# Bias-tile loads, last-pair store tiles and one product's place at the seam between a projection stage and an attention stage

## The chip, the cores and the metric

The kernel runs on 1 core of one Trainium2 chip. The metric is the time of one execution on the device, in microseconds (us). Engines are named as in the profile: PE multiplies matrices, DVE and ACT work elementwise, POOL issues software DMAs (and does a little elementwise work), SP issues hardware DMAs. Each engine runs its instructions in the order in which they stand in its program; a semaphore wait at the head stops everything behind it on that engine.

## The reference, cut to what matters

A transformer block on 1024 tokens of width 1024, all in float32. One projection makes every input of two mixers and the merge gates; the second mixer (NSA) is attention in three branches with a relative-position bias.

```python
u = rms_norm(h, g_norm_mix[l])
proj = jnp.einsum('btd,de->bte', u, w_in[l]) + b_in[l]        # 1024 x 5408
mq, mk, mv, mo, mi, mf, nq, nkv, ngate, merge = split_columns(proj, IN_SIZES)
y_m = mlstm_mixer(mq, mk, mv, mo, mi, mf, ...)
y_n = nsa_mixer(nq, nkv, ngate, pe_cmp[l], w_cmp1[l], w_cmp2[l], rel_bias)
...
# in nsa_mixer, per block of queries:
lc = q @ kc_ + table[rel_bucket(t - cmp_end)];   p_c = masked_softmax(lc, ...)
ls = q @ k_g + bias_s;                           p_s = masked_softmax(ls, ...)
lw = q @ k_wb + table[rel_bucket(dist)];         p_w = masked_softmax(lw, mask_w)   # window of 512
out = gb[0] * (p_c @ vc_) + gb[1] * (p_s @ v_g) + gb[2] * (p_w @ v_wb)
...
gates = jax.nn.sigmoid(merge); mixed = jnp.sum(gates * branch, axis=2)
```

## The kernel before, in words

Activations and weights are split into a high and a low float32r part, and each product is three matmuls (lines 351 to 353: high by high, high by low, low by high). The normalised, transposed activations lie in two tiles, `UTH` and `UTL`.

**The projection stage** makes 128-column tiles of the projection in pairs (the table `PAIRS`, numbered 0 to 11; pairs 10 and 11 are merge gates 0 to 3). A pair is computed by a seven-product 2x2 block scheme: products 1 to 7, in the order 1, 6, 2, 7, 4, 5, 3. The left operand is a block of `UTH`/`UTL` or one of four operands derived from them. Products 1, 2, 3 read blocks in place, 5, 6, 7 read the derived operands in the T tiles, and product 4 reads the fourth derived operand, which has been written over one quarter of `UTH`/`UTL`; the quarter's own values wait in DRAM (`d_b12`) and are loaded back by POOL (line 1335, eight loads of 256 KB) once the last product 4, that of pair 11, has been read. The right operand is a weight block or a sum of them, prepared by ACT (high part, line 723) and DVE (low part, line 494) into a ring of four operand tiles `op0` to `op3`. Raw weights come through a ring of three tiles `rp0` to `rp2`. A product takes 12 matmuls and one of eight PSUM banks (`bk0` to `bk7`); the results are evicted in the order of the products: product 1 by ACT (line 779), the others by DVE (lines 776 and 786), into the pair's two 1024-column destination tiles. For pairs 7 to 11 these are the tiles S0 and S1. Once complete they are stored to DRAM by SP: pair 9 to `d_qh`/`d_ql` (lines 1040 and 1041), pairs 10 and 11 to `d_mg` (line 1045).

The order of the work in this stage is set by a planner (`Plan`): steps with reads, writes, costs and a rank are put greedily on the engines, and a step that raises its `boost` goes ahead. `preps` prepares operands some products ahead of the one that is planned, in the order of `plist`. `compress` (four weight tiles in S4 to S7, lines 1211 to 1248) runs between the products.

**The seam.** While the last products run, the attention stage's inputs are loaded: by POOL the queries (S4, S5), keys (S8, S9 and R10) and values, by SP the bias tiles of the first pair of heads (`load_f`, line 1301: S6 and S7, 1024 columns each, from `d_rep`). `first_merge` prepares the first merge weight tile for the next stage (line 1346 load, 1349 and 494 split). After the plan the windowed bias tiles `FW0` and S2 (640 columns each) are loaded by SP.

**The attention stage** has 32 units (a pair of heads and a block of 128 queries), in an order written out by its own scheduler, filled up with merge products (`d`, lines 351 to 353). Logits of a unit go to one of two PSUM tiles `S` (lines 1430 and 1431); DVE adds the bias and takes the row minimum (line 1457, `E...<-S...`), which frees the PSUM tile; ACT takes the exponential (1461); DVE scales (1482); PE transposes (1512); ACT and DVE split (1517, 1521); PE multiplies by the values (1532, 1534). Unit 0 (query block 0) reads S6 and S7; unit 1 (query block 7) reads `FW0` and S2 first.

Of the kernel before, what the change touches and what calls it, by code (L numbers as in the profile page):

```python
# [8 lines left out]
F32 = mybir.dt.float32  # L9
# [5 lines left out]
P = 128  # L15
T = 1024
# [15 lines left out]
FX = 1152  # L32
# [140 lines left out]
def body(ctx, tc, a, out):  # L173
    nc = tc.nc
# [48 lines left out]
    S = {n: Region(bigp, f"S{n}", 1024, F32R if n < 2 or n > 3 else F32) for n in (0, 1, 4, 5, 6, 7, 8, 9)}  # L223
# [9 lines left out]
    def slot(n):  # L233
        return S[n]() if n < 10 else R10()[:, 1024 * (n - 10):1024 * (n - 9)]
# [56 lines left out]
    d_mg = [tc.dram_tile([P, T], F32, name=f"d_mg{j}") for j in range(16)]  # L291


    class Stream:
# [12 lines left out]
        def dma(self, upto):  # L307
            while self.nd <= min(upto, len(self.jobs) - 1):
                src, (n, m), _ = self.jobs[self.nd]
                t = self.pool.tile([P, T], F32, name=f"raw{self.nd}", tag="raw", bufs=self.bufs)  # L310
                v = t[:, 0:n * m].rearrange("p (n m) -> p n m", n=n)
                col = 0
                for s in (src if isinstance(src, list) else [src]):
                    w = s.shape[-1]
                    nc.sync.dma_start(v[:, :, col:col + w], s)
                    col += w
                self.raw[self.nd] = v
                self.nd += 1
# [76 lines left out]
    def fm_tile(n, psp, dtag, dbufs, evict, pool=False, deep=False, mark=False):  # L395

        wh, wl = ws.get(n)
        for r in range(2):
            ps = psp.tile([P, 512], F32, name=f"d{n}_{r}", tag=dtag, bufs=dbufs)
            for k in range(KT):  # L400
# [51 lines left out]

    PAIRS = [("qk", 0), ("kw", 0), ("qk", 1), ("cv", 0), ("qk", 2), ("o", 0), ("qk", 3), ("nq", 0),
             ("o", 2), ("nq", 2), ("mg", 0), ("mg", 2)]
    DSLOT = [11, 0, 11, 0, 11, 0, 11, 0, 0, 0, 0, 0]
    HSLOT = {1: lambda r: slot(6 + r), 7: lambda r: slot(11 + r), 9: lambda r: (RND, RMV)[r]()[:, 0:1024]}
    HKEY = {1: lambda r: keys_of(6 + r), 7: lambda r: keys_of(11 + r), 9: lambda r: [("ND", "MVH")[r]]}
    DBI = {"qk": lambda j: j, "o": lambda j: 4 + j // 2, "cv": lambda j: 6, "kw": lambda j: 7,
# [49 lines left out]
    def sbuf(*ns):  # L508
        return pl.buf([k for n in ns for k in keys_of(n)], True)
# [289 lines left out]
    LAST = NPR - 1  # L799
    SEQ = {n: [(n, q) for q in (1, 6, 2, 7, 4, 5, 3)] for n in range(NPR)}  # L800
# [1 line left out]
    SEQ[1] = [(1, q) for q in (6, 7, 4, 5, 3)]  # L802
    SEQ[LAST] = [(LAST, q) for q in (4, 1, 6, 2, 7, 5, 3)]
    plist = [x for n in range(NPR) for x in SEQ[n]]
    made = []

    def preps(upto):
        while len(made) < min(upto, len(plist)):
            n, q = plist[len(made)]
            prep(n, q)  # L810
            made.append((n, q))
            if q == 3:
                load_raw(n + 2, 0)
            for m in (n, n + 1):
                if (m, 1) in made and (m == 0 or (m - 1, 3) in made) and (m, 3) not in SB_:
                    for s in (1, 2, 3):
                        sums(m, s)
                    load_raw(m + 1, 1)
# [104 lines left out]
    for t in (1, 2, 3):  # L923
        for j in range(4):
            x = pl.buf([("T", t, j)], True)
# [15 lines left out]
    for j in range(4):  # L941
        b = tf1[j]
# [3 lines left out]
    for j in range(4):  # L946
        b = tf2[j]
# [3 lines left out]
    for j in range(4):  # L951
        tsplit(1, j, f1(j), tf1[j])
        b = tf1[j]
# [3 lines left out]
    for j in range(4):  # L957
        b = tf2[j]
# [13 lines left out]
    drep = pl.buf((), True)  # L972
# [17 lines left out]
    dkc, dkk, dym = pl.buf((), True), pl.buf((), True), pl.buf((), True)  # L990
    dqq = [pl.buf((), True) for _ in range(4)]
    dmg = pl.buf((), True)
# [31 lines left out]
    def finish(n):  # L1024
        nm, j = PAIRS[n]
        d = DST[n]
        rows_ = [[d[r, 0], d[r, 1]] for r in range(2)]
        if nm == "qk":
            pl.boost = -60
            conv(n)  # L1030
            pl.boost = 0
        elif nm in ("kw", "nq"):
            for r in range(2):
                v = lambda r=r: slot(DSLOT[n] + r)
                hb, hi = pl.buf(HKEY[n](r), True), lambda r=r: rnd(HSLOT[n](r))
                dh, dl = (d_kh[r], d_kl[r]) if nm == "kw" else (d_qh[j + r], d_ql[j + r])
                tok = dkk if nm == "kw" else dqq[j + r]
                step1("ACT", 1000.0, lambda hi=hi, v=v: nc.scalar.activation(hi(), v(), AF.Copy), rows_[r], [hb])
                ew(ANY2, lambda v=v: rnd(v()), v, lambda hi=hi: cast32(hi()), ALU.subtract, [hb], rows_[r])
                dma(lambda dh=dh, hi=hi: nc.sync.dma_start(dh, cast32(hi())), [hb], [tok])  # L1040
                dma(lambda dl=dl, v=v: nc.sync.dma_start(dl, v()), rows_[r], [tok])
        else:
            for r in range(2):
                d_ = {"cv": d_kc[r], "o": d_so[(j + r) % 4], "mg": d_mg[j + r]}[nm]
                dma(lambda d_=d_, r=r: nc.sync.dma_start(d_, slot(DSLOT[n] + r)), rows_[r], [dkc] if nm == "cv" else [dmg])


    def head(h):
# [206 lines left out]
    fbt = lambda r: S[6 + r]()  # L1255
# [39 lines left out]

    def load_f(p, r, w, eng):
        h = 2 * p + r
        t_, o_, n_ = (fbt(r), 127, T) if not w else (FWT(r), FX + 127, 640)
        (FW if w else FB)[h] = t_
        d_ = d_rep[h][0:1, :]  # L1300
        eng.dma_start(t_, bass.AP(tensor=d_.tensor, offset=d_.offset + o_, ap=[[RW - 1, P], [1, n_]]))
# [15 lines left out]
    def first_loads():  # L1317
# [9 lines left out]
        dma(lambda: load_f(0, 1, 0, nc.sync), [drep], [b[7]])  # L1327
        gl(4, lambda: load_k(0, 0, gq), [dkk], [b[8], b[9]])

    def last_loads():  # L1330
        nd, mv, sm = pl.buf(["ND"], True), pl.buf(["MVH"], True), pl.buf([("ss", z) for z in range(2)] + [("CN", z) for z in range(3)], True)
        for z, b in ((1, nd), (2, mv), (3, sm)):
            gl(1, lambda z=z: load_v(z), [dvh], [b])
        for j in range(4):
            gl(2, lambda j=j: [nc.gpsimd.dma_start(FS[4][z][:, :, j], d_b12[z][:, :, j]) for z in range(2)], [db12], tb[4, j])
        b = sbuf(3)
        gl(1, lambda: load_v(0), [dvh], [b])
        gl(1, lambda: load_v(4), [dvh], [pl.buf((), True)])
# [21 lines left out]
    for n in range(NPR):  # L1360
        for x in SEQ[n]:
            pl.boost = 80
            preps(plist.index(x) + 4)
            pl.boost = 0
            product(*x)
            if x[1] == 3:
                if n == 0:
                    rel_rows()
                finish(x[0])
                nm, j = PAIRS[x[0]]  # L1370
                if nm == "qk":
                    head(j)
        if n == 8:
            compress()
        if n == LAST - 1:
            first_loads()
# [15 lines left out]
    with ExitStack() as sc:  # L1392
        cp = sc.enter_context(tc.tile_pool(name="stC", bufs=1, reuse_waits="tile"))
        psC = sc.enter_context(tc.tile_pool(name="psC", bufs=1, space=PSUM, reuse_waits="tile"))
        FWT = {0: cp.tile([P, 640], F32, name="FW0"), 1: S[2]()}.__getitem__
        for r in range(2):
            load_f(0, r, 1, nc.sync)


        def c_dense():  # L1400
# [319 lines left out]
        while any(queues.values()):  # L1720
            best = None
            for e in queues:
                cand = None
                for op in queues[e][:LOOK[e]]:
                    r = ready(op, e)
# [74 lines left out]
    with ExitStack() as se:  # L1800
# [32 lines left out]
        for d in range(8):  # L1833
            n = j_br[d]
# [155 lines left out]
    for i in range(NT):  # L1990
        b = piece(16 + i)
# [252 lines left out]
    for gi, pairs in enumerate(GROUPS):  # L2244
# [6 lines left out]
        for q in QS:  # L2251
            ps = [pl.buf() for _ in range(4)]
            for p in pairs:
                (a11, a21), (a12, a22) = ra[p, 0], ra[p, 1]
                (b11, b12), (b21, b22) = rb[p, 0], rb[p, 1]
                if q == 7:
# [3 lines left out]
                    x, y = s3, t3  # L2260
                elif q == 5:
                    into(SUM, a21, a21, a22, ALU.add, [a22])
                    into(SUM, b12, b12, b11, ALU.subtract, [b11])
                    x, y = a21, b12
                elif q == 6:
                    into(SUM, a11, a21, a11, ALU.subtract, [a21])
                    into(SUM, b11, b22, b12, ALU.subtract, [b22, b12])
                    x, y = a11, b11
                elif q == 4:
                    into(SUM, b21, b21, b11, ALU.subtract, [b11])  # L2270
                    x, y = a22, b21
                elif q == 3:
                    into(SUM, a12, a12, a11, ALU.subtract, [a11])
                    x, y = a12, b22
                else:
                    x, y = (a11, b11) if q == 1 else (a12, b21)
# [22 lines left out]
    n = 0  # L2299
# [4 lines left out]
    for r in (1, 0):  # L2304
        for j in range(4):
            i = 2 * j + r
# [69 lines left out]
```

## Time and profile before

| | us |
|---|---|
| median of 3 runs | 1574.69 (1571.67 to 1578.49) |
| the profiled execution's own time | 1576.46 |
| its span in the profile | 1574.7 |
| PE busy | 1529.6 (97%) |
| DVE busy | 1175.1 (75%) |
| ACT busy | 782.0 (50%) |
| POOL busy | 126.7 (8%) |

In the profile's times the projection stage ends and the attention stage begins at about 377 us. Between 335 and 400 us PE is busy for 59.36 of 65 us at a mean granted clock of 0.95; from 400 to 680 us, the rest of the attention stage, it is busy for 279.08 of 280 us at 1.00.

How to read the rows: in a timeline a row is the start, the duration, the engine, line, operation, output<-input, and in brackets the idle time of the engine before it with what ended that. A matmul's duration contains its latency; back to back they start 0.23 us apart at full clock. "SPq" and "POOL ... DMA_DIRECT2D" rows are the issue of a DMA, not its transfer.

### The profile page before, as it was taken

What the parts mean: (1) busy time and instruction counts of PE and PEld (TensorE: products, weight loads), DVE (VectorE), ACT (ScalarE), POOL (GpSimd) and SP (SyncE); (2) the same over time, 40 slices, a digit from 0 to 9 for tenths busy, and PEclk for the clock granted to TensorE, in tenths of its full rate; (3) what the DMA queues carried; (4) which work ended last, traced back from release to release, by engine and by line L of the source; (5) the groups of instructions that cost most, each with busy time, mean ns of one, the idle gap of its engine ahead of it and who ended that gap; (6) DMA issues with size and microseconds to landing.
All of it is one profiled execution on the core that took longest, in us unless ns stands there. A gap on an engine that the chain in (4) does not pass through costs nothing.

```text
span 1574.7 us, 22067 instructions
## 1 busy us (share of the span) xinstructions
PE 1529.6 (97%) x7714; PEld 1291.2 (82%) x7714; DVE 1175.1 (75%) x2467; ACT 782.0 (50%) x1668; POOL 126.7 (8%) x184
## 2 busy tenths in 40 slices
PE   6999999998999999998999999999999999999998
PEld 5877888886989888986888888888888888888876
DVE  6978888855888688856564597666666666978996
ACT  6325665653788688865443253333333333454443
POOL 2000000022111211001000041000000000000120
PEclk9999999999999999999999999999999999999999
DMA  8424655599142914137556222222322223650202
GB/s 272 125 75 135 214 182 155 176 241 233 40 112 54 172 40 113 48 101 254 153 176 206 75 67 87 80 81 84 132 92 81 81 88 127 253 215 0 107 1 107
DMA packets 162839, 198.21 MB, mean 126 GB/s; under 512 B 9944, under 2 KB 121974, under 8 KB 162728
## 3 DMA queue, kind: packets, MB, share of 16 engines
q1 hardware_dynamic: 150840, 183.06, 36.5%
q0 software_dynamic: 11600, 13.09, 5.0%
q8 instruction: 61, 1.00, 0.3%
q10 hardware_dynamic: 288, 0.66, 0.1%
q14 instruction: 50, 0.41, 0.1%
HBM read 146.34 MB, written 58.29 MB: 130 GB/s over the span
## 4 chain that ended last, share of the span: by engine, by line
PE 85%; DVE 7%; DMA 5%; ACT 2%; issue 1%; SPq 0%; POOL 0%; DVEq 0%; ACTq 0%; POOLq 0%
PE PS L352 15%; PE PS L353 15%; PE PS L351 15%; PE bk L351 4%; PE bk L352 4%; PE bk L353 4%; PE T L1512 4%; PE obank L1534 2%; PE d L351 2%; PE obank L1532 2%; PE d L353 2%; PE d L352 2%; PE br L353 2%; PE br L351 2%; PE br L352 2%; DMA d_ql<-S 1%
## 5 line engine op out<-in xcount | busy, mean ns | idle before, releaser
L1877 DVE TENSOR_TENSOR sl<-PS,sl 128x512 f32<-128x512 f32 x182 | 123.0, 687 | 99.7 <-PE PS L353 97.7
L1521 DVE TENSOR_TENSOR TL<-T,TH 128x512 fp32r<-128x512 f32 (+1 forms) x184 | 103.3, 582 | 29.1 <-ACT TH L1517 28.3
L1517 ACT ACTIVATE TH<-T 128x512 fp32r<-128x512 f32 (+1 forms) x184 | 90.2, 510 | 28.7 <-PE T L1512 25.7
L1880 ACT ACTIVATE sl<-sl 128x512 f32<-128x512 f32 (+1 forms) x85 | 53.3, 631 | 71.7 <-PE PS L352 46.3
L1877 DVE TENSOR_TENSOR sl<-sl,sl 128x512 f32<-128x512 f32 (+1 forms) x111 | 75.2, 686 | 15.4 <-ACT sl L1880 11.8
L351 PE MATMUL bk<-UTH,op 128*128 128x512 f32 x192 | 77.5, 403 | 1.6 <-ACT S L779 1.6
L1880 ACT ACTIVATE wh<-sl 128x512 fp32r<-128x512 f32 x61 | 38.5, 631 | 81.5 <-PE PS L352 69.1
L353 PE MATMUL bk<-UTH,op 128*128 128x512 f32 x192 | 75.1, 391 | 0.0
L352 PE MATMUL bk<-UTL,op 128*128 128x512 f32 x192 | 75.0, 391 | 0.0
L351 PE MATMUL d<-UTH,whi 128*128 128x512 f32 x176 | 71.9, 409 | 1.4 <-ACT mg L1387 0.7
L353 PE MATMUL d<-UTH,wlo 128*128 128x512 f32 x176 | 69.3, 394 | 1.4 <-POOL wlo L333 1.4
L352 PE MATMUL d<-UTL,whi 128*128 128x512 f32 x176 | 69.1, 393 | 0.0
L351 PE MATMUL PS<-q 128*128 128x512 f32 x172 | 67.0, 390 | 0.0
L352 PE MATMUL PS<-q 128*128 128x512 f32 x172 | 67.0, 390 | 0.0
L353 PE MATMUL PS<-q 128*128 128x512 f32 x172 | 67.0, 390 | 0.0
L1880 ACT ACTIVATE q<-sl 128x512 fp32r<-128x512 f32 x74 | 43.3, 624 | 45.9 <-PE PS L352 30.1
L351 PE MATMUL bk<-T,op 128*128 128x512 f32 x144 | 58.3, 405 | 0.0
L353 PE MATMUL bk<-T,op 128*128 128x512 f32 x144 | 56.4, 391 | 0.0
L352 PE MATMUL bk<-T,op 128*128 128x512 f32 x144 | 56.3, 391 | 0.0
L351 PE MATMUL br<-YH,whi 128*128 128x512 f32 x128 | 50.8, 397 | 2.2 <-ACT whi L331 2.2
L353 PE MATMUL br<-YH,wlo 128*128 128x512 f32 x128 | 50.8, 397 | 2.2 <-POOL wlo L333 2.2
L1877 DVE TENSOR_TENSOR wh<-sl,wh 128x512 fp32r<-128x512 f32 x58 | 39.7, 685 | 15.3 <-ACT wh L1880 15.3
(1377 smaller groups left out, 4854.6 us busy)
## 6 DMA issues: line engine op xcount, KB each, us to landing
rp<-in_w_in SPq DMA_DIRECT2D x22, 512.0 KB, 4.6
ra<-in_w_gate SPq DMA_DIRECT2D x22, 512.0 KB, 4.0
d_gu<-sl SPq DMA_DIRECT2D x44, 256.0 KB, 2.0
q<-d_mg SPq DMA_DIRECT2D x32, 256.0 KB, 2.9
d_rep<-d_row SPq DMA_DIRECT2D x8, 960.0 KB, 7.4
sl<-d_gu SPq DMA_DIRECT2D x15, 512.0 KB, 5.3
sl<-in_w_down SPq DMA_DIRECT2D x15, 512.0 KB, 4.3
ra<-in_w_up SPq DMA_DIRECT2D x11, 512.0 KB, 3.5
```

What stands on the lines that cost most here:

```text
L351: nc.tensor.matmul(ps, ah, bh, start=first, stop=False)
L352: nc.tensor.matmul(ps, ah, bl, start=False, stop=False)
L353: nc.tensor.matmul(ps, al, bh, start=False, stop=last)
L1512: nc.tensor.transpose(pt[:, z, P * r:P * r + P], e, ident)
L1517: nc.scalar.activation(hl[0][:, 0:m], pt[:, 0:m], AF.Copy)
L1521: nc.vector.tensor_tensor(hl[1][:, 0:m], pt[:, 0:m], cast32(hl[0])[:, 0:m], ALU.subtract)
L1532: nc.tensor.matmul(po, vv, th[:, z, :], start=(st[1] == 0), stop=False)
L1534: nc.tensor.matmul(po, vv, tl[:, z, :], start=False, stop=(st[1] == st[2]))
L1877: return pl.step(alts, lambda e: ENG[e].tensor_tensor(out_(), x(), y(), alu), reads, writes, **kw)
L1880: return pl.step((("ACT", cost),), lambda e: nc.scalar.activation(out_(), x(), fn), reads, writes, **kw)
```

## The change

- The destination tiles of pair 10 become S6 and S7 (they were S0 and S1), so that pairs 10 and 11 write to separate tiles.
- Product 4 of pair 11 is placed behind product 4 of pair 10, ahead of products 5 and 3 of pair 10. The order in which operands are prepared stays.
- The S2 bias load moves into the plan, ahead of the value loads and the restore in the program's text; `FW0` is still requested after the plan.
- The stores of pair 11 to `d_mg` leave the plan and are issued behind the `FW0` load.

```diff
-    DSLOT = [11, 0, 11, 0, 11, 0, 11, 0, 0, 0, 0, 0]
+    DSLOT = [11, 0, 11, 0, 11, 0, 11, 0, 0, 0, 6, 0]
...
     plist = [x for n in range(NPR) for x in SEQ[n]]
-    made = []
+    SEQ[LAST - 1][5:] = [(LAST, 4), (LAST - 1, 5), (LAST - 1, 3)]
+    SEQ[LAST] = SEQ[LAST][1:]
+    made, run = [], set()
...
                 d_ = {"cv": d_kc[r], "o": d_so[(j + r) % 4], "mg": d_mg[j + r]}[nm]
-                dma(lambda d_=d_, r=r: nc.sync.dma_start(d_, slot(DSLOT[n] + r)), rows_[r], [dkc] if nm == "cv" else [dmg])
+                if n < LAST:
+                    dma(lambda d_=d_, r=r: nc.sync.dma_start(d_, slot(DSLOT[n] + r)), rows_[r], [dkc] if nm == "cv" else [dmg])
...
-        t_, o_, n_ = (fbt(r), 127, T) if not w else (FWT(r), FX + 127, 640)
+        t_, o_, n_ = (fbt(r), 127, T) if not w else (FWT[r](), FX + 127, 640)
...
+    FWT = {}
+
     def last_loads():
+        b = sbuf(2)
+        FWT[1] = lambda: S[2]()
+        dma(lambda: load_f(0, 1, 1, nc.sync), [drep], [b], kb=320.0)
...
-            preps(plist.index(x) + 4)
+            preps(next(i for i, y in enumerate(plist) if y not in run) + 4)
+            run.add(x)
...
-        FWT = {0: cp.tile([P, 640], F32, name="FW0"), 1: S[2]()}.__getitem__
+        fw0 = cp.tile([P, 640], F32, name="FW0")
+        FWT[0] = lambda: fw0
+        load_f(0, 0, 1, nc.sync)
         for r in range(2):
-            load_f(0, r, 1, nc.sync)
+            nc.sync.dma_start(d_mg[PAIRS[LAST][1] + r], slot(DSLOT[LAST] + r))
```

What this does to SP's queue at the seam, from the last store of pair 9 on (`rp` are raw weights, `d_mg` the stores of the merge pairs, `d_rep` the bias). Before:

```order
L1041 DMA d_ql2_137<-S0_1_1163 128x1024
L1301 DMA S6_1_1165<-d_rep0_112 128x1024
L1301 DMA S7_1_1167<-d_rep1_113 128x1024
L1355 DMA rp2_203<-in_w_in 128x8x128
L1045 DMA d_mg0_185<-S0_1_1163 128x1024
L1045 DMA d_mg1_186<-S1_1_1289 128x1024
L1346 DMA rp0_201<-in_w_in 128x8x128
L1045 DMA d_mg2_187<-S0_1_1163 128x1024
L1045 DMA d_mg3_188<-S1_1_1289 128x1024
L1301 DMA FW0_3120<-d_rep0_112 128x640
L1301 DMA S2_0_99<-d_rep1_113 128x640
```

Changed:

```order
L1043 DMA d_ql2_137<-S0_1_1163 128x1024
L1363 DMA rp2_203<-in_w_in 128x8x128
L1048 DMA d_mg0_185<-S6_1_1165 128x1024
L1354 DMA rp0_201<-in_w_in 128x8x128
L1304 DMA S2_0_99<-d_rep1_113 128x640
L1048 DMA d_mg1_186<-S7_1_1167 128x1024
L1304 DMA S6_1_1165<-d_rep0_112 128x1024
L1304 DMA S7_1_1167<-d_rep1_113 128x1024
L1304 DMA FW0_3119<-d_rep0_112 128x640
L1408 DMA d_mg2_187<-S0_1_1163 128x1024
L1408 DMA d_mg3_188<-S1_1_1289 128x1024
```

The S6 and S7 bias loads have moved from the head of this stretch to behind the stores of pair 10, which now leave from the same two tiles; the two windowed bias loads stand ahead of pair 11's stores.

On ACT, the eviction of pair 10's product 1 (line 779) around the end of `compress` (table loads, then a SiLU and the eviction to `VHC`). Before:

```order
L1233 ACT_TABLE_LOAD
L1233 ACTIVATE R10_0_102<-bk2_230 128x126
L1234 ACT_TABLE_LOAD
L723 ACTIVATE op3_239<-rp0_201 128x512
L779 ACTIVATE S0_1_1163<-bk3_231,COLS_85 128x4x128
L723 ACTIVATE op0_236<-rp2_203 128x512
L1247 ACTIVATE VHC_82<-bk7_235 63x2x64
```

Changed:

```order
L779 ACTIVATE S6_1_1165<-bk3_231,COLS_85 128x4x128
L1236 ACT_TABLE_LOAD
L1236 ACTIVATE R10_0_102<-bk2_230 128x126
L1237 ACT_TABLE_LOAD
L723 ACTIVATE op3_239<-rp0_201 128x512
L723 ACTIVATE op0_236<-rp2_203 128x512
L1250 ACTIVATE VHC_82<-bk7_235 63x2x64
```

The eviction stands four rows earlier and writes another tile; what stood behind it (`op0`, `VHC`) no longer does.

## The prediction

> **What bounds the kernel now.** The shares of the page come first, then the windows around the place that the change touches.
>
> ```profile
> PE 1529.6 (97%) x7714; PEld 1291.2 (82%) x7714; DVE 1175.1 (75%) x2467; ACT 782.0 (50%) x1668; POOL 126.7 (8%) x184
> 335.00:400.00 65.00, 59.36 (x283) 48.39 (x282) 33.27 (x91) 25.76 (x60) 17.67 (x32) 0.95 1.11 226
> 400.00:680.00 280.00, 279.08 (x1864) 251.15 (x1862) 232.31 (x764) 229.85 (x610) 39.33 (x86) 1.00 0.35 81
> 390.00:395.00 5.00, 4.78 (x14) 3.93 (x15) 3.37 (x12) 3.46 (x10) 0.00 (x0) 0.50 0.01 3
> ```
>
> PE is the bound, and at the seam it idles 65 - 59.36 = 5.6 us and runs for some microseconds at a granted clock of 0.50 (the first of the two figures after the engines). That is about all that an edit here can win. Behind the seam PE is busy for 279.08 of 280 us, so what PE gains by 400 us should reach the end. The DMA share of 1.11 says that the transfers at the seam are queued up. The timeline of PE shows the idle places:
>
> ```profile
> 355.77 0.39 PE L353 MATMUL bk<-UTH,op 128*128 128x512 f32 x1
> 357.77 0.50 PE L351 MATMUL bk<-UTH,op 128*128 128x512 f32 x1 [1.60 <-ACT S L779]
> ...
> 376.75 0.39 PE L353 MATMUL bk<-UTH,op 128*128 128x512 f32 x1
> 377.69 0.51 PE L351 MATMUL d<-UTH,op 128*128 128x512 f32 x1 [0.54 <-ACT op L1349]
> 378.03 0.39 PE L352 MATMUL d<-UTL,op 128*128 128x512 f32 x1
> 378.95 0.50 PE L353 MATMUL d<-UTH,op 128*128 128x512 f32 x1 [0.53 <-DVE op L494]
> ...
> 386.88 0.40 PE L353 MATMUL d<-UTH,op 128*128 128x512 f32 x1
> 390.22 0.76 PE L1430 MATMUL S1s<-S,S 128*128 128x512 f32 x1 [2.94 <-DVE nx L1457]
> 390.78 0.63 PE L1431 MATMUL S1s<-S,S 128*128 128x512 f32 x1
> 391.21 0.63 PE L1430 MATMUL S1s<-S,S 128*128 128x512 f32 x1
> ...
> 396.32 0.22 PE L1430 MATMUL S2w<-R,S 128*128 128x128 f32 x1
> ```
>
> Start to start, less the 0.23 us of a matmul: 2.00 - 0.23 = 1.77 us, 0.94 - 0.23 = 0.71, 0.92 - 0.23 = 0.69, 3.34 - 0.23 = 3.11. From 390.22 to 396.32 matmuls start 0.43 us apart instead of 0.23, which costs 6.10 x (1 - 0.23/0.43) = 2.84. Together 9.1 us. The chain of waits names what is behind them:
>
> ```profile
> 335.42 21.52 DMA d_ql<-S
> 357.03 0.70 ACT S L779
> ...
> 365.79 10.68 DMA rp<-in_w_in
> 376.58 1.07 ACT op L1349
> 377.67 1.24 DVE op L494
> ...
> 382.81 6.12 DMA FW<-d_rep
> 389.06 0.73 DVE E1w L1457
> ```
>
> Three transfers, then: pair 9's last store, which holds S0 while pair 10's first eviction wants it; the first merge weights; and the `FW0` bias, which SP requests at 382.81, behind pair 11's stores.
>
> **The change, part by part.** *Separate tiles, 1.77 us.* Pair 10's product 1 is evicted to S6, which `compress` has read last at 340.88 + 3.74 = 344.6 at the latest. Its 0.7 us on ACT fall ahead of the table load, into the 0.99 us of idle time in the second row here, so they cost nothing; without that cover they would delay `compress`'s second half by 0.7 us.
>
> ```profile
> 340.88 3.74 PE L1216 MATMUL bk<-S,S 128*128 128x126 f32 x32
> 344.65 0.28 ACT L1233 ACTIVATE R<-bk 128x126 f32<-128x126 f32 x1 [0.99 <-PE bk L1216]
> 371.33 0.69 ACT L779 ACTIVATE S<-bk,COLS 128x512 f32<-128x512 f32 x1 [7.34 <-DMA d_mg<-S]
> ...
> 342.86 2.11 SPq L1301 DMA_DIRECT2D S<-d_rep  x2
> 360.45 0.38 SPq L1355 DMA_DIRECT2D rp<-in_w_in  x1
> 363.83 0.84 SPq L1045 DMA_DIRECT2D d_mg<-S  x2
> ...
> 381.71 0.80 SPq L1045 DMA_DIRECT2D d_mg<-S  x2
> ```
>
> All banks then come free while DVE is idle, and the 1.77 us go. Pair 11 still writes to S0, but its product 1 now ends at about 361.4, some 4 us behind the landing of pair 9's store (335.42 + 21.52 = 356.9), and the 7.34 us that ACT waits for `d_mg` there, in the third row, vanish too.
>
> *Product 4 sooner.* The same 12 matmuls stand two products (2 x 12 x 0.23 = 5.5 us) earlier. Its operand is ready, since the preparation order stays. POOL's restore of the quarter starts when it ends, about 353 instead of 361.12. In the program no row of PE up to 390 reads the quarter, so this is worth 0 on PE by itself; what it does is to take the restore's 2 MB out of the way of the bias loads sooner.
>
> *First merge weights, 1.40 us.* `rp0` is free when pair 11's product 2 is prepared, about 360 now, behind pair 10's product 3 (356.0 + 2.7 for the product put ahead of it, + 0.8 for the eviction = 359.5). Hardware-queue transfers moved from 360.45 (`rp`) to 376.47 (`rp`) 4 x 512 KB in 16.0 us, 4.0 us per 512 KB. One store and `rp0` thus land at about 367.5, and 2.3 us of splitting make 370; even with its whole old 10.68 us it is 373.3. PE arrives at 376.98 - 1.77 = 375.2. Both waits (0.71 + 0.69) go, with 2 us or more of cover.
>
> *`FW0` and S2 ahead of the stores, 5.8 us.* DVE has done unit 0 at 385.60 + 0.48 = 386.08 (last row of the next fence). PE started 390.22 - 389.06 = 1.16 us after DVE's `E1w`, so it can start at 387.24, against 387.11 without any wait: 0.1 of the 3.11 us stays. The clock then does not fall, and its 2.84 us go as well. In the stretch at half clock DVE was busy for 3.37 of 5 us, so 4.1 of 6.10 us, and PE's full-rate 3.26 us are less than that; DVE will have begun this work earlier, so I charge nothing and keep 0.8 us for the range. Sum so far: 1.77 + 1.40 + 3.0 + 2.84 = 9.0 us.
>
> *The price: S6 and S7 late.* They were requested at 342.86 and landed long before use. Now they are requested only when pair 10's stores have left the same tiles. SP waits in order: store 0 at 359.5, `rp0`, S2 (which waits for pair 11's operand of product 5, about 362.8), store 1 at 363.3. Ahead of and with store 1 the queue holds 3 x 512 + 320 KB; at 4.0 us per 512 KB it has landed at 359.5 + 14.5 = 374. S7 is requested then, and behind that wait stand `FW0` and pair 11's stores on SP. The first needs are these, 1.77 + 1.40 = 3.2 us sooner in the change:
>
> ```profile
> 381.75 0.29 DVE L1457 CUSTOM_DVE_ANT_0 E0w<-S0w,S 128x128 f32<-128x128 f32 x1
> ...
> 382.24 0.29 DVE L1457 CUSTOM_DVE_ANT_0 E0w<-S0w,S 128x128 f32<-128x128 f32 x1
> ...
> 385.60 0.48 DVE L1482 TENSOR_SCALAR E0s<-E0s,rs 128x128 f32<-128x128 f32 x2
> ```
>
> So S6 by 378.6, S7 by 379.1, `FW0` by 382.9. How long does S7 take from its request? The bounds are the rows of the same kind of load:
>
> ```profile
> S<-d_rep SPq DMA_DIRECT2D x2, 512.0 KB, 16.0
> FW<-d_rep SPq DMA_DIRECT2D x1, 320.0 KB, 6.1
> UTH<-d_b POOLq DMA_DIRECT2D x4, 256.0 KB, 11.4
> 361.12 0.78 POOL L1335 DMA_DIRECT2D UTH<-d_b  x1 [7.41 <-PE bk L353]
> DMA to landing us min/median/max: 4.4/7.6/16.0
> ```
>
> With the DMA engines free 4.4 us (378.4, no wait); amid full queues 16.0 us (390, 11 us late). I take 6.3 us, near the `FW<-d_rep` row, which also had stores queued ahead of it (1 MB, at 381.71) and the restore behind it: 380.4, that is 1.3 us late. PE waits that long for a PSUM tile of unit 0, too short for the clock (the 1.60 us wait above left it at full rate). `FW0`, 320 KB, follows S7 by some 2 us, 382.4, and is needed at 382.9 + 1.3: covered by 1.8 us. Pair 11's stores have no reader before the merge: 0 us.
>
> [...]
>
> Net: 9.0 - 1.3 = 7.7 us. The profiled execution took 1576.46 us, 1.77 above the median of the runs shown; 1576.46 - 7.7 = 1568.8, and at the median's level **1567.0 us**, 0.49% faster. About 0.5%, 7.9 us, is what a measurement of this kernel can tell from no change, so the forecast lies on that edge.
>
> **The rivals.** *A: all in time.* S7 lands within 5.1 us of its request, by 379.1: 9.0 us, 1565.7. For it: 1 MB of S6 and S7 no longer sits in the queue at 342.86, so what is behind it, keys and `rp`, lands sooner, and the 4.4 us. Against it: the DMA share of 1.11.
>
> *B: the stall moves.* S7 or `FW0` comes 3 to 6 us late; at 3.5 PE idles about as long as it does now at 387, the clock falls again for 2.84 us, and 9.0 - 3.5 - 2.84 = 2.7 us are left: 1572.0. For it: restore, `d_mg` and bias all want the DMA engines at 365 to 380.
>
> [...] In this trace 2.94 us were enough, so the measurement decides: I let B begin at 3 us.
>
> *C: slower.* One mechanism: SP's wait for store 1 to land before it may request S7. If S7 then takes the 16.0 us of the row above, it lands at 390, 11 us late; 9.0 - 11 - 2.84 = -4.8, 1579.5. It decides from a landing at 379.1 + 6.2 = 385.3 on, 11.3 us behind the request. Against it: the 16.0 us were met in a queue whose store of 335.42 was itself 21.52 us under way; here only S6, 512 KB, is ahead.
>
> *D: the change does not do what it says.* `FW0` is still requested behind something late: instead of pair 11's stores it is SP's wait for store 1. Should that store land only at 379.6 (382.81 less the 3.2 us), `FW0` is requested no sooner for PE than now, and only 1.77 + 1.40 = 3.2 us are won: 1571.5. Against it: that is 16 us for a store at 363.3, and the stores of 363.83 had landed when ACT went on at 371.33.
>
> **How the numbers follow.** Forecast (a gain of 6 to 8.7 us, 1566.0 to 1568.7): 0.47. A: 0.21. B and D together: 0.25. C: 0.07. Faster by over 0.5%: nearly all of A and under half of the forecast, 0.20 + 0.20 = 0.40. Slower by over 0.5% needs C at its worst, most of its 0.07: 0.05. Within: 0.55. The range takes in A and B with 2 us either side for a median of a few runs: 1562.5 to 1574.0.
>
> **What would show it.** Right: no wait of PE for ACT line 779 near 356; no wait of the first `d` matmuls for `op`; `E1w` no longer waiting for `FW<-d_rep`; the clock at 1.00 through the seam; a wait of 0 to 3 us of the first `E0w` rows for `S<-d_rep`; the span shorter by what PE no longer idles. Wrong: an idle PE of 3 us or more near 380 with a clock of 0.50 behind it (B, C); a new wait of SP ahead of `FW0` (D); or a full gain at 400 us that is not there at 680.

## The result, and the profile after

| | before | after |
|---|---|---|
| median, us | 1574.69 (1571.67 to 1578.49) | 1566.17 (1565.21 to 1568.24) |
| the profiled execution's own time, us | 1576.46 | 1565.54 |
| its span, us | 1574.7 | 1563.8 |

The ratio is 0.9948, with a 95% interval of 0.9933 to 0.9962: 8.2 us less (6.0 to 10.5). The forecast was 1567.0 us, 7.7 us less. The size is right. Most of its parts are not, as the experiments show.

The window of the kernel after, in the columns of the windows of before (busy time of PE, PEld, DVE, ACT, POOL, then granted clock, DMA share, GB/s):

```profile
335.00:400.00 65.00, 63.90 (x340) 53.84 (x340) 40.42 (x116) 32.13 (x78) 18.10 (x33) 1.00 1.06 226
```

PE idles 1.1 us at the seam instead of 5.6, and the clock is 1.00 throughout. The timeline of PE has one idle place left:

```profile
349.66 0.44 PE L1246 MATMUL bk<-R 128*63 128x64 f32 x4
...
379.21 0.39 PE L353 MATMUL d<-UTH,op 128*128 128x512 f32 x1
380.70 0.30 PE L1441 MATMUL S0s<-S,S 128*128 128x128 f32 x1 [1.10 <-DVE nx L1468]
...
390.77 1.03 PE L1523 MATMUL T<-cst,E1w 128*128 128x128 f32 x8
...
687.66 0.38 PE L1545 MATMUL obank<-TL,RMV 128*128 128x256 f32 x1
```

The first row here is the start of `compress`'s value product, the row of 390.77 unit 1's transposes, and the last one the last matmul of the attention stage. In before the same three are:

```profile
350.04 0.44 PE L1243 MATMUL bk<-R 128*63 128x64 f32 x4
...
399.53 1.03 PE L1512 MATMUL T<-cst,E1w 128*128 128x128 f32 x8
...
696.33 0.39 PE L1534 MATMUL obank<-TL,RMV 128*128 128x256 f32 x1
```

I call the time from the first to the second the **seam length**: 399.53 - 350.04 = 49.49 us before, 390.77 - 349.66 = 41.11 after, 8.38 less. To the end of the attention stage it is 346.29 against 338.00, 8.29 less, so nearly all of it is kept. What follows from there to the end of the span (1574.7 - 696.33 = 878.4 us, after 876.1) is code that the change does not touch, and it differs from one execution to the next by some microseconds: two profiled executions of one kernel of the experiments took 878.6 and 874.1 there. So below the seam length, read from each kernel's trace, tells the kernels apart, and the whole times only confirm it.

The chain of waits of after names the last idle place (start, duration, what):

```profile
362.79 10.84 DMA d_mg<-S
...
373.71 6.33 DMA S<-d_rep
...
380.17 0.29 DVE E0w L1468
```

That is the price of the late S7, link by link: store 1 leaves at 362.79, lands at 373.6, S7 is requested behind it and lands at 380.0. And the queue of SP, with the rows of DVE and ACT that decide when pair 11's stores can leave:

```profile
359.26 0.32 SPq L1048 DMA_DIRECT2D d_mg<-S  x1
359.86 0.38 SPq L1354 DMA_DIRECT2D rp<-in_w_in  x1
362.42 0.32 SPq L1304 DMA_DIRECT2D S<-d_rep  x1
362.79 0.91 SPq L1048 DMA_DIRECT2D d_mg<-S  x1
367.39 6.64 SPq L1304 DMA_DIRECT2D S<-d_rep  x2
374.33 0.32 SPq L1304 DMA_DIRECT2D FW<-d_rep  x1
376.24 0.81 SPq L1408 DMA_DIRECT2D d_mg<-S  x2
```

```profile
371.10 1.06 ACT L1357 ACTIVATE op<-rp 128x1024 fp32r<-128x1024 f32 x1 [6.72 <-DMA rp<-in_w_in]
```

```profile
372.20 1.22 DVE L494 TENSOR_TENSOR op<-rp,op 128x1024 fp32r<-128x1024 f32 x1 [2.02 <-ACT op L1357]
373.34 2.87 DVE L776 TENSOR_TENSOR S<-bk,S 128x512 f32<-128x512 f32 x4
...
383.10 0.82 DVE L1468 CUSTOM_DVE_ANT_0 E1w<-S1w,FW 128x640 f32<-128x640 f32 x1
```

Here is a thing that the prediction overlooked. DVE splits the first merge weights (line 494) and only then makes pair 11's last four evictions (line 776), and pair 11's stores leave right behind these: at 376.24. They leave some 5 us sooner than in before not because of their own place on SP but, as the experiments bear out, because `rp0` was there at 371. In before the same two DVE rows read:

```profile
357.75 1.42 DVE L776 TENSOR_TENSOR S<-bk,S 128x512 f32<-128x512 f32 x2 [9.19 <-ACT S L779]
...
365.04 0.69 DVE L494 TENSOR_TENSOR S<-rp,S 128x512 f32<-128x512 f32 x1
...
377.67 1.23 DVE L494 TENSOR_TENSOR op<-rp,op 128x1024 fp32r<-128x1024 f32 x1 [3.07 <-ACT op L1349]
378.81 2.87 DVE L776 TENSOR_TENSOR S<-bk,S 128x512 f32<-128x512 f32 x4
```

So the reading to be tested: the idle places of before are links of one chain. Pair 9's store holds S0; ACT's eviction waits for it; DVE idles 9.19 us behind ACT, until 357.75, and then works off a heap of evictions, so that its last read of `rp0`'s old content comes only at 365.04; `rp0` is requested at 365.79, the split comes at 377.67, the last evictions at 378.81, the stores at 381.71, and `FW0` behind them.

### The profile page after: what moved, and what is told of

It reads as the page before. It is cut to its first block, busy times and chain, and to the rows that moved or that the text cites. A ratio compares the mean times of both kernels' runs of the same rounds, so it can differ in the third digit from the quotient of the medians.

```text
span 1563.8 us, 22061 instructions
## 1 busy us (share of the span) xinstructions
PE 1521.2 (97%) x7714; PEld 1284.8 (82%) x7714; DVE 1174.9 (75%) x2467; ACT 782.4 (50%) x1668; POOL 127.2 (8%) x184
## 4 chain that ended last, share of the span: by engine, by line
PE 87%; DVE 6%; DMA 4%; ACT 2%; issue 1%; SPq 0%; POOL 0%; DVEq 0%; ACTq 0%; POOLq 0%
PE PS L352 15%; PE PS L353 15%; PE PS L351 15%; PE bk L351 5%; PE bk L352 5%; PE bk L353 5%; PE T L1523 4%; PE obank L1545 2%; PE obank L1543 2%; PE d L351 2%; PE d L353 2%; PE d L352 2%; PE br L353 2%; PE br L352 2%; PE br L351 2%
```

## Experiments

Each kernel is timed against the kernel before on the same chip; ratios are given with their 95% intervals. "rp0" is the request of the first merge weights, counted from the start of the value product (the first mark of the seam length).

| kernel | rp0, us from the mark | seam length, us | ratio to before |
|---|---|---|---|
| before | 15.75 | 49.49 | 1 |
| product order alone | 15.32 | 49.59 | 1.0016 (1.0006 to 1.0027) |
| after, without separate tiles | 15.13 | 48.49 | 0.9993 (0.9984 to 1.0001) |
| rp0 ahead of the stores alone | 15.08 | 47.87 | 0.9997 (0.9985 to 1.0009) |
| separate tiles alone | 15.65 | 47.00 | 1.0000 (0.9985 to 1.0015) |
| after, without product order | 15.71 | 45.30 | 0.9974 (0.9964 to 0.9985) |
| bias loads ahead of stores alone | 16.08 | 43.62 | 0.9980 (0.9968 to 0.9992) |
| after | 10.20 | 41.11 | 0.9948 (0.9933 to 0.9962) |
| after, timed again | 10.20 | 41.15 | 0.9964 (0.9950 to 0.9978) |
| after, stores ahead of FW0 | 10.20 | 41.04 | 0.9966 (0.9951 to 0.9981) |
| after, S2 load last | 10.20 | 40.60 | 0.9955 (0.9940 to 0.9969) |
| separate tiles, rp0 ahead of S6 | 10.80 | 40.12 | 0.9936 (0.9922 to 0.9950) |
| the same, timed again | 10.80 | 39.84 | 0.9960 (0.9944 to 0.9975) |
| after, second row's store first | 10.20 | 39.76 | 0.9951 (0.9935 to 0.9968) |

The seam length repeats well: 41.11 and 41.15 us for after, 40.12 and 39.84 for the kernel that was also timed twice. It falls into two groups by when `rp0` goes out: 10.2 to 10.8 us from the mark gives 39.8 to 41.2, and 15.1 to 16.1 gives 43.6 to 49.6.

### Separate tiles alone

```diff
-    DSLOT = [11, 0, 11, 0, 11, 0, 11, 0, 0, 0, 0, 0]
+    DSLOT = [11, 0, 11, 0, 11, 0, 11, 0, 0, 0, 6, 0]
```

> The kernel before with one edit: pair 10 writes to S6 and S7. Seam length means: from the start of the first value product of the compress step to the start of unit 1's transposes of its window part; 49.49 us before, 41.11 after the whole change. SP now has rp0 behind the S6 bias load, which waits for the landing of pair 10's store. Theory P (the sum on record: separate tiles give 1.77 us, the order of FW0 ahead of the stores gives 5.84): only the idle place near 356 goes, FW0 is still requested behind pair 11's stores and late, the clock falls to 0.50 again, and rp0, requested some 8 us later than before, lets the first merge weights come 3 us or more later: seam 47 to 51 us, total within 3 us of before (1572 to 1577). Theory Q (the tiles themselves free pair 11's evictions of the 7.34 us wait, so its stores leave at about 377 and FW0 is requested at about 378 instead of 382.81): no stretch at 0.50 behind unit 0, seam 42 to 45 us, total about 1568 to 1571, or less if rp0 is late.

SP's timeline, then PE's:

```profile
356.33 0.80 SPq L1045 DMA_DIRECT2D d_mg<-S  x2
364.67 0.32 SPq L1301 DMA_DIRECT2D S<-d_rep  x1
365.10 0.38 SPq L1346 DMA_DIRECT2D rp<-in_w_in  x1
...
381.57 0.79 SPq L1045 DMA_DIRECT2D d_mg<-S  x2
```

```profile
377.55 0.50 PE L351 MATMUL d<-UTH,op 128*128 128x512 f32 x1 [2.93 <-ACT op L1349]
...
389.94 0.47 PE L1430 MATMUL S1s<-S,S 128*128 128x512 f32 x1 [1.87 <-DVE nx L1457]
```

The wait near 356 is gone and pair 10's stores leave some 7 us sooner than in before. But the planner has put the S6 load ahead of `rp0`; it waits for the landing of the store from S6 (364.67), and `rp0` goes out at 365.10, as late as ever. PE waits 2.93 us for the merge weights, its clock falls there (0.51 from 378 to 380), and pair 11's stores leave at 381.57. Both theories named a part: P the late `rp0`, and the seam of 47 us; but Q's premise that freed evictions make the stores early is false, and P's stretch at 0.50 behind unit 0 did not come: 1.87 us of idle time were left there, and behind them the clock stayed at 1.00. In this kernel DVE had read `rp0`'s old content by 360.19 (a row of 359.50 and 0.69 us): the tile was free 4.9 us before its request.

### Bias loads ahead of the stores alone

Pair 11's stores leave the plan and stand behind the `FW0` load, S2 is loaded in `last_loads`; tiles and product order as before.

```diff
-                dma(lambda d_=d_, r=r: nc.sync.dma_start(d_, slot(DSLOT[n] + r)), rows_[r], [dkc] if nm == "cv" else [dmg])
+                if n < LAST:
+                    dma(lambda d_=d_, r=r: nc.sync.dma_start(d_, slot(DSLOT[n] + r)), rows_[r], [dkc] if nm == "cv" else [dmg])
...
     def last_loads():
+        b = sbuf(2)
+        FWT[1] = lambda: S[2]()
+        dma(lambda: load_f(0, 1, 1, nc.sync), [drep], [b], kb=320.0)
...
+        load_f(0, 0, 1, nc.sync)
         for r in range(2):
-            load_f(0, r, 1, nc.sync)
+            nc.sync.dma_start(d_mg[PAIRS[LAST][1] + r], slot(DSLOT[LAST] + r))
```

> The kernel before with one edit: S2 and FW0 are requested ahead of pair 11's stores; pair 10 stays on S0 and S1. Theory P (order of the loads is worth 5.84 us by itself): the idle places near 356 (1.77) and at the first merge products stay, FW0 lands before 383, unit 1 does not wait for it, no stretch at 0.50: seam 43.7 us, total about 1569. Theory Q (the stores of pair 11 were late because of their tiles; with S0 and S1 still shared, pair 11's evictions are still held until about 371 and DVE does not come to unit 0 sooner): FW0 is early here too, so the 5.8 us are won all the same, and the two edits overlap: each alone gives most of the gain. Rival R: the earlier requests for 640 KB delay the rp load and the stores on the same queue, and PE waits 1 to 3 us longer for the first merge weights: seam 45 to 47 us.

SP's timeline, the windows and PE's timeline:

```profile
376.82 0.32 SPq L1302 DMA_DIRECT2D FW<-d_rep  x1
```

```profile
360.00:364.00 4.00, 4.00 (x13) 3.14 (x12) 3.90 (x8) 0.83 (x2) 0.56 (x1) 0.64 2.75 182
```

```profile
358.54 0.50 PE L351 MATMUL bk<-UTH,op 128*128 128x512 f32 x1 [1.93 <-ACT S L779]
```

With `rp0` and the last evictions as late as in before (16.08 us from the mark for `rp0`), the order of `FW0` and the stores is worth 5.87 us of seam: theory P's figure of 5.8. It is so although the wait near 356 here was 1.93 us instead of 1.60 and the clock fell behind it (0.64 from 360 to 364, the window above). PE, delayed by that, came to the merge weights when they were there. The two differences about cancel, so that the agreement to 0.1 us is in part chance.

### Product order alone

```diff
+    SEQ[LAST - 1][5:] = [(LAST, 4), (LAST - 1, 5), (LAST - 1, 3)]
+    SEQ[LAST] = SEQ[LAST][1:]
...
-            preps(plist.index(x) + 4)
+            preps(next(i for i, y in enumerate(plist) if y not in run) + 4)
+            run.add(x)
```

> The kernel before with one edit: product 4 of pair 11 stands two products sooner. Theory P: worth 0 on PE by itself; the restore starts at about 353 to 356 instead of 361.12; idle places near 356 and 387 and the stretch at 0.50 stay: seam 49.5 us, total within 2 us of before. Rival: the restore's 2 MB now run against pair 9's store, the rp2 load and pair 10's stores, and these land later: the waits for S0 and for op grow by 1 to 3 us, seam 50.5 to 52.5. Other rival: out of the way of FW0 sooner, the restore lets FW0 land in 4.4 instead of 6.12 us: seam 47.8, and 2.8 less if the clock holds.

```profile
382.31 0.50 PE L353 MATMUL d<-UTH,op 128*128 128x512 f32 x1 [3.60 <-DVE op L494]
```

Worth nothing by itself, as theory P said, but for another reason: not because nothing moved. The 3.34 us gap at 387 shrank and one of 3.60 us, the row of PE here, took its place at the merge weights. The first rival's growing waits are there, and they cost what the place behind gave back. That they came from the restore's transfers, as this rival had it, the run does not show. About 2.1 of the 3.60 us are the split itself: its row on DVE (378.96) lasts 3.30 us, against 1.23 in before, beside work of POOL's (see the last section).

### After, stores ahead of FW0

```diff
-        load_f(0, 0, 1, nc.sync)
         for r in range(2):
             nc.sync.dma_start(d_mg[PAIRS[LAST][1] + r], slot(DSLOT[LAST] + r))
+        load_f(0, 0, 1, nc.sync)
```

> The kernel after with one edit: pair 11's stores are issued ahead of the FW0 load again. After, the stores were ready at 376.24 and FW0 was requested at 374.33. Theory P (the order is what won 5.84 us): FW0 is queued behind 1 MB of stores, which take 8 us at 4.0 us per 512 KB, lands at 385 to 386 against a need at 383.1, PE idles 2 to 3 us and the clock falls: seam 43 to 47 us, total 1568 to 1572. Theory Q (with separate tiles the stores are early and the order hardly matters): FW0 is requested at 377.1, lands 6.1 to 6.5 us later at 383.2 to 383.6, PE idles 0 to 0.5 us, no stretch at 0.50: seam 41.1 to 41.7, total within 1 us of after (1566.2).

```profile
375.78 0.89 SPq L1407 DMA_DIRECT2D d_mg<-S  x2
376.96 0.44 SPq L1304 DMA_DIRECT2D FW<-d_rep  x1
```

```profile
382.86 0.82 DVE L1468 CUSTOM_DVE_ANT_0 E1w<-S1w,FW 128x640 f32<-128x640 f32 x1 [0.25 <-PE T L1523]
```

Within the change the order of these loads is worth nothing: the seam is 41.04 against 41.11. `FW0` is requested at 376.96 behind 1 MB of stores and is there at 382.86, when DVE comes to it (it waited 0.25 us for PE, not for the load). Theory Q holds. The prediction's largest term, 5.84 us, is therefore not what this edit does in the company of the others; something else had already made the stores early.

### After, without the product order

The product order's two edits undone in after.

> The kernel after with one part undone: product 4 of pair 11 is back behind pair 10's products. With the separate tiles alone (run before this one) the first merge weights' tile rp0 was requested at 365.10, PE waited 2.93 us for op at 377.55 and its clock fell; FW0 was still behind pair 11's stores at 382.67. SP's queue here has rp0 behind the S6 load, which waits for pair 10's store to land. Theory P (product 4's place is worth 0 on PE): seam about 41 to 42 us, total 1566 to 1568. New theory N (the change won because rp0 goes out at 359.86 instead of 365.79, and it does only with the product's new place): rp0 at about 365, op at about 377.5, idle 2 to 3 us and a stretch at 0.50 around 380, but FW0 early, no second wait at 388: seam 45 to 47 us, total about 1570 to 1572.

SP's and PE's timelines:

```profile
365.23 0.32 SPq L1302 DMA_DIRECT2D S<-d_rep  x1
365.65 0.38 SPq L1352 DMA_DIRECT2D rp<-in_w_in  x1
```

```profile
377.96 0.50 PE L351 MATMUL d<-UTH,op 128*128 128x512 f32 x1 [2.86 <-ACT op L1355]
```

Without the product order 4.19 us of the 8.38 go: `rp0` is behind the S6 load again, PE waits 2.86 us and its clock falls (0.50 from 380 to 382). The new theory N gave 45 to 47, and 45.30 came. The edit that the prediction put at 0 is worth half the gain, and not through POOL's restore, but through SP: with the products in the new order the planner lets store 0 and `rp0` go one behind the other at 359.3 and 359.9, ahead of the loads that must wait for stores. The kernel with `rp0` ahead of S6, below, settles that it is SP: it has the old product order and a restore that starts only at 359.55 (353.36 in after), and loses nothing.

### After, without separate tiles

`DSLOT` of before in after.

> The kernel after with one part undone: pair 10 writes to S0 and S1 again. SP: S6 and S7 early, rp2, store 0, rp0, S2, store 1, FW0, pair 11's stores. Theory P: the 1.77 us near 356 come back, the 1.26 us wait for S7 goes, the rest of the gain stays: seam 41.6 to 42, total about 1567. Theory N: pair 11's evictions into S0 and S1 wait for pair 10's stores again, the split of the first merge weights and the last evictions stand behind them on DVE, PE idles 3 us and more at the first d matmuls as with the product order alone (3.60 us there): seam 45 to 49, total 1570 to 1574, though FW0 is early.

DVE's and PE's timelines:

```profile
379.25 0.75 DVE L786 SCALAR_TENSOR_TENSOR S<-bk,DB,S 128x512 f32<-128x512 f32 x1 [3.81 <-DMA d_mg<-S]
379.92 2.21 DVE L494 TENSOR_TENSOR op<-rp,op 128x1024 fp32r<-128x1024 f32 x1
```

```profile
382.18 0.80 PE L353 MATMUL d<-UTH,op 128*128 128x512 f32 x1 [3.63 <-DVE op L494]
```

7.38 us of 8.38 go. The separate tiles had 1.77 us in the prediction. Pair 11's evictions wait for pair 10's stores again: ACT's into S0 for 8.66 us, until 372.83, and then DVE's of 379.25 for 3.81 us. The merge weights' split stands behind that one on DVE, begins at 379.92 though ACT had the high part ready at 377.67, and takes 2.21 us instead of 1.22.

### rp0 ahead of the stores alone

In before, pair 10's two stores are made to depend, in the planner, on the `rp0` load, so that it stands ahead of them on SP.

```diff
-        dma(lambda: nc.sync.dma_start(v8(b.ap), src), (), [b])
+        first = dma(lambda: nc.sync.dma_start(v8(b.ap), src), (), [b])
+        for s in hold:
+            s.deps.add(first)
```

(`hold` is the list of these two stores.)

> The kernel before with one edit: the rp0 load stands ahead of pair 10's two stores on SP, tiles as before. Theory N in its strong form (only rp0's request matters): rp0 at about 360.8, split by 373, DVE's last evictions early, FW0 requested at 378 or before, the 0.50 stretch gone: seam 43 to 44 us (the 1.77 us near 356 stay), total about 1569. Rival T (the shared tiles matter as much): pair 10's stores land later behind rp0, ACT's eviction into S0 goes on at 374 or later instead of 371.33 and DVE's work behind it with it; PSUM banks come free late, PE idles 3 us or more near 375, total 1573 to 1577.

```profile
365.34 0.38 SPq L1350 DMA_DIRECT2D rp<-in_w_in  x1
```

```profile
357.29 1.42 DVE L776 TENSOR_TENSOR S<-bk,S 128x512 f32<-128x512 f32 x2 [8.50 <-ACT S L779]
...
364.58 0.69 DVE L494 TENSOR_TENSOR S<-rp,S 128x512 f32<-128x512 f32 x1
```

Its place on SP was not what held `rp0` in before: first in the queue, it still goes out only at 365.34, when DVE has read the tile's old content (364.58 + 0.69 = 365.27). DVE is so late since it idled 8.50 us behind ACT's eviction into S0. The strong form of N falls: the shared tile comes first, and `rp0` follows from it. Of rival T the late eviction into S0 came (ACT goes on at 376.04) and the total, but PE's wait near 378 is 1.71 us and not 3.

### Separate tiles, and rp0 one place earlier

The separate tiles alone, and in the planner the S6 and S7 loads depend on the `rp0` load (the diff shown last, with these two loads in `hold`). Product order, `FW0` and pair 11's stores as in before.

> The kernel before with the separate tiles and the rp0 load one place earlier on SP, ahead of the S6 load that waits for pair 10's store; product order and the order of FW0 and pair 11's stores as before. With the tiles alone rp0 was requested at 365.10 and the total was that of before. Theory N: rp0 is requested at about 360, op is ready before PE needs it, DVE's last evictions end at about 376, pair 11's stores leave then and FW0 lands in time: seam 41 to 42.5 us, total within 2 us of after, nearly the whole gain without the other two parts. Theory P (FW0 must stand ahead of the stores: 5.84 us): the stretch at 0.50 behind unit 0 stays, seam 46 us or more, total 1571 or more.

SP's timeline and the window:

```profile
361.21 0.38 SPq L1348 DMA_DIRECT2D rp<-in_w_in  x1
...
376.33 1.03 SPq L1045 DMA_DIRECT2D d_mg<-S  x2
377.66 0.53 SPq L1301 DMA_DIRECT2D FW<-d_rep  x1
```

```profile
335.00:400.00 65.00, 64.77 (x349) 54.95 (x348) 41.17 (x117) 32.23 (x78) 18.66 (x35) 1.00 1.04 228
```

Two small edits give a seam 1 us shorter than the whole change, 40.12 against 41.11, and below theory N's 41 to 42.5; PE is busy for 64.77 of 65 us. `rp0` goes out at 361.21, as soon as DVE has read the tile's old content (a row of 360.46 and 0.69 us), and everything behind follows: pair 11's stores at 376.33, `FW0` behind them at 377.66, in time. This separates the theories: the reading above is shown, from its first link (the shared tile) over `rp0` to `FW0`.

### Beside after once more

After itself, timed with the next three:

> The kernel after, unchanged, timed beside the next three on one chip, so that they can be compared with it and not only with the kernel before. Expected: 0.993 to 0.996 of before, seam 41.1 us with the wait of 1.26 us for S7's bias near 380.

It came to 0.9964, with a seam of 41.15: 5.7 us less than before, where the first comparison had 8.2. The intervals overlap from 0.9950 to 0.9962.

The kernel with tiles and `rp0`, again:

> The kernel before with separate tiles and rp0 one place earlier, timed once more beside after. Theory N (both kernels let rp0 go out at 360 to 361; this one asks for S6 and S7 sooner and has no wait for them): seam 40.1 against 41.1 us, so 1 us or 0.06% below after, too little to be told by times; 1564 to 1567. Rival: the product order and the order of FW0 bring something that the seam does not show; then after is faster by more than 2 us.

Seam 39.84. Its median was 1565.31 us against 1567.52 of after, but the intervals of their ratios (0.9944 to 0.9975, 0.9950 to 0.9978) overlap; that it is faster than after is shown by the seam alone.

After with the S2 load behind `FW0`:

```diff
-        b = sbuf(2)
-        FWT[1] = lambda: S[2]()
-        dma(lambda: load_f(0, 1, 1, nc.sync), [drep], [b], kb=320.0)
...
         load_f(0, 0, 1, nc.sync)
+        load_f(0, 1, 1, nc.sync)
```

> The kernel after with one edit: the S2 bias load goes behind FW0, so pair 10's second store is not held by S2's wait on SP. After, that store left at 362.79, S7 was requested at 373.7 and landed 2.0 us after DVE wanted it; PE idled 1.26 us. Theory (SP's order holds the store by 2.5 us): store at about 360.3, S7 requested at 371 to 372, landed by 378, no idle PE near 380: seam 39.8 to 40.2, total within noise of after, about 1 us less. Rival (the DMA queues are full then, the store lands at 373 or 374 all the same): the wait stays at 1 us, seam 41. Second rival: S2 lands too late for unit 1, which needs it at 384.4: a new wait near 385.

```profile
360.85 0.64 SPq L1048 DMA_DIRECT2D d_mg<-S  x1
368.09 5.64 SPq L1304 DMA_DIRECT2D S<-d_rep  x2
```

```profile
380.21 0.29 DVE L1468 CUSTOM_DVE_ANT_0 E0w<-S0w,S 128x128 f32<-128x128 f32 x1 [1.50 <-DMA S<-d_rep]
```

Half a miss: counted from the mark, store 1 leaves 2.5 us sooner (10.64 against 13.13), but the two bias issues that wait for the stores end at 368.09 + 5.64 = 373.73, only 0.8 us sooner (23.52 against 24.37), and DVE waits 1.50 us instead of 2.00. Most of what the store gained in the queue it lost on the way, as the rival said. The seam, 40.60, is 0.5 us shorter, little more than the 0.3 us by which two traces of one kernel differ.

After with the second row's store of pair 10 first, ahead of `rp0`:

```diff
-            for r in range(2):
+            for r in ((1, 0) if n == LAST - 1 else (0, 1)):
```

> The kernel after with one edit: of pair 10's two stores the second row's goes first, since its values are complete first, ahead of rp0. Theory: it leaves at about 357.5, lands by 368, S7 is requested then; S6 follows when the other store has landed at about 371, and lands at 377 to 378: no idle PE near 380, seam 39.8 to 40.3. Rival: the store now ahead of rp0 lets rp0 land 2 to 4 us later than 371, DVE's split and last evictions move to 375 to 379 and PE waits for op again: seam 41 to 44, total 1 to 3 us above after.

```profile
357.41 0.32 SPq L1048 DMA_DIRECT2D d_mg<-S  x1
```

```profile
335.00:400.00 65.00, 65.00 (x352) 55.32 (x351) 41.31 (x118) 32.55 (x79) 18.96 (x35) 1.00 1.03 228
```

Here the store leaves some 6 us sooner (from the mark), before `rp0` and the S2 load; the wait for S7 is gone and PE idles nowhere between 335 and 400 us. Seam 39.76, 1.35 us below after, close to the 1.26 us that PE idles in after. By time it cannot be told from after (0.9951, 0.9935 to 0.9968).

## Why the prediction was right, and where not

**The sum.** Of the four losses that it counted all are gone: 1.77 + 1.40 + 3.11 + 2.84 = 9.1 us. The price is the gap at 379.21, 1.49 - 0.23 = 1.26 us; 9.1 - 1.26 = 7.9 us, against 7.7 predicted and 8.38 measured on the seam. The last 0.5 us these places do not explain.

**The price of S6 and S7** was right in each link: store 1 at 362.79 (363.3 predicted), landed at 373.6 (374), S7 at 380.0 (380.4), 1.26 us of idle time (1.3), the clock at 1.00. That the 6.3 us came so close is in part luck: they were picked between 4.4 and 16.0 us from the row of a 320 KB load, and the 4.4 us too are those of a 320 KB load (`FW`, at 608.9), while S7 has 512 KB. The restore was unfinished when S7 was requested, at 373.71: its last load left at 364.36 and took 13.2 us.

**First merge weights.** `rp0` was requested at 359.86 (about 360), but took until 371.10 instead of 367.5, near the bound with its old 10.68 us; the split ended at 373.42, and PE had 1.2 us of cover left (its first `d` matmul is at 374.66) instead of 2 or more.

**Separate tiles, 1.77 us.** This step failed in its attribution. It priced only the idle place at 357.77 and put no price on DVE's delay behind the same wait; the earlier `rp0` that follows from it was counted as a step of its own. The 9.19 us for which DVE stood still there is what made `rp0`, the split, the last evictions, the stores and `FW0` late. Undoing this part alone costs 7.38 us.

**`FW0` and S2 ahead of the stores, 5.8 us.** The places and the 5.84 us are right, and alone the edit is worth 5.87 us. As a part of the change it is worth nothing (41.04 against 41.11), because the stores are early anyway. What failed is that I took pair 11's stores at 381.71 as given and did not ask what DVE did ahead of them. The split at 377.67 is in the prediction's chain, but only as a wait of PE; that the last evictions, at 378.81, stand behind it was not in the working.

**Product 4 sooner, 0 by itself.** Right alone (49.59 against 49.49), wrong in the change: without it 4.19 us are lost. I argued from the operands and from POOL, and did not ask what SP's order would be without this edit. The request of `rp0` at about 360 was read from SP's order in the whole change; that it needs this edit was not seen.

So the parts do not add: alone they give 2.49, -0.10 and 5.87 us; undone one at a time the first two cost 7.38 and 4.19, and of the third its main part, the place of `FW0`, costs nothing. The total came out right because each place of the sum was read from PE's own idle time and the clock, and these do not depend on which edit clears them. It held only because all of them were cleared, and for that the edit put at 0 was needed: without it the seam is 45.30. To that extent the total came out right by luck.

**The rivals.** Neither B nor C came; D's condition did not arise (`FW0` was requested at 374.33). A, no price at all, is what the store of the second row first gives.

## What to carry to other kernels

Read back an idle chain to its first link before pricing the links apart: a store that holds a destination tile also delayed the reader of a ring buffer, and through it the next request, the next split and the next store. Where several edits cut one chain, cost each with the others in place and with the others gone; the sum of the idle places holds as long as all of them are cleared, its division among the edits does not. And where a planner sets a queue's order, a new wait (here a load that waits for a store from its own tile) belongs behind the requests that are free to go sooner: that one place was worth 47.00 - 40.12 = 6.9 us of seam.

## What the runs showed of the hardware

**How much idle time lets the clock fall.** At the seam, waits of PE of 1.10, 1.60, 1.71, 1.76 and 1.87 us were followed by a clock of 1.00, and those of 1.93, 2.67, 2.86, 2.93, 2.94, 3.60 and 3.63 us by a stretch near 0.50. The prediction let the fall begin at 3 us, which is too late. The seam's waits alone look like a boundary near 1.9 us, but behind the seam the same traces show that there is no such boundary: a wait of 1.87 us in before (at 1528.52) was followed by a clock of 0.51, and one of 1.93 us in after (at 819.88) by 1.00. The clearest pair is one matmul in the two executions of the kernel with separate tiles and `rp0` ahead of S6, the first execution first:

```profile
1519.90 0.52 PE L352 MATMUL PS<-q,wh 128*128 128x512 f32 x1 [1.90 <-DVE q L1881]
```

```profile
1516.00 0.50 PE L352 MATMUL PS<-q,wh 128*128 128x512 f32 x1 [1.90 <-DVE q L1881]
```

After the first the clock was 0.50 from 1520.9 to 1523, after the second 1.00 throughout. From this row to the end of the span it is 46.1 us in the first and 44.5 in the second, a part of the difference of 4.5 us between these two executions behind the attention stage. So for waits of 1.87 to 1.93 us the length alone does not decide; what does is not shown.

**A store requested sooner landed little sooner.** With the S2 load last, store 1 was requested 2.5 us sooner from the mark and S7's request behind it came 0.8 us sooner, as the section on that kernel shows; requested ahead of `rp0`, at 357.41, it no longer held anything up. Why is not shown; only `rp0` and store 0 had been requested just ahead of it in the first of these, and S2 as well in after.

**A split on DVE beside POOL's work took longer.** DVE's split of the first merge weights takes 1.22 us in after. With the product order alone it takes 3.30 us, and in after without separate tiles 2.21. In these two POOL splits the next merge weights (line 333) at the same time, from 378.84 to 381.18 and from 378.70 to 381.04. The two rows lie beside each other for 2.2 and 1.1 us, and DVE's is longer by 2.1 and 1.0. In after POOL's row begins at 374.97, behind the end of DVE's split at 373.42. That POOL's work is the cause is argued from these times alone; no run here separates the two.
